# Another order of the projection products in the recurrence, twelve sums moved to GpSimd, and tiles laid out anew

## The chip, the cores and the metric

The kernel runs on one core of a Trainium2 chip. The metric is the device time of one execution in microseconds (us), of which the median of several runs is given. TensorE (PE) does matrix products, ScalarE (ACT) copies, casts and activations, VectorE (DVE) sums and products of tiles, GpSimd (POOL) a few of the same, and SyncE (SP) issues transfers. Each engine works off its own list of instructions in order; the engines meet at semaphores.

## The reference

A decoder trunk of two layers, 1024 positions of 1024 features, all float32. Cut to the part that the change touches:

```python
def hgrn2_mixer(h, w_in, lower_bound, g_norm_w, w_out):     # layer 0; 8 heads of 128
    q, f, i, g = jnp.split(h @ w_in, 4, axis=-1)            # w_in is 1024 x 4096
    fg = lb + (1.0 - lb) * jax.nn.sigmoid(heads(f))
    o = hgrn2_chunkwise(jax.nn.silu(heads(q)), 1.0 - fg, heads(i), jnp.log(fg))
    o = o * lax.rsqrt(jnp.mean(jnp.square(o), -1, keepdims=True) + RMS_EPS)
    o = o * g_norm_w * jax.nn.silu(heads(g))
    return o.reshape(B, S, D) @ w_out
...
    for layer in range(DEPTH):                              # DEPTH = 2
        mix = hgrn2_mixer(...) if layer == 0 else swa_sink_mixer(...)
        h = layer_norm(ALPHA * h + mix, ...)
        h = layer_norm(ALPHA * h + conv_ffn(h, ...), ...)
```

`hgrn2_chunkwise` is the recurrence: per head a state of 128 x 128 is decayed by `fg`, takes in key times value and is read by the query. The keys are `1 - fg`, the values are `i`, the gate is `g`.

## The kernel before

The program runs through the layers in stages: the projections and the recurrence of layer 0 (to about 500 us), its FFN, the shared keys and values with the attention of layer 1, and the second FFN. A float32 product is made of three TensorE matmuls: each operand is split into a high part (a cast on ScalarE) and a low part (the operand less its high part, `low_part`, L197), and `mm3` issues high x low, low x high and high x high as L222, L223 and L224.

**Head 0** is projected straight (values and gate at L777/L778, added up at L748 and L750). **Heads 1 to 7** are projected by a Strassen-Winograd scheme. The four projections of a head are taken in two pairs: m = 0 to 13 stands for (head, g), where g = 0 is the pair of queries and forget gates and g = 1 that of values and gates. The 1024 positions are cut into an early and a late half, and so are the features that are summed over. Each pair takes seven products P1 to P7, written (m,p), each 12 matmuls of 128x512. P2 goes to PSUM bank 1, P5 and P3 to bank 2, and P1, P6, P7 and P4 to bank 3*(m mod 2), where each of them is added onto what the bank holds. P6, P7, P3 and P4 are therefore put onto a bank that holds the product before them, and the scheme wants that product's value as well: it must be read out first. This is the work of `evacuate`: ScalarE copies P1 (L1360), P6 (L1362), P5 (L1364) and, for g = 1, P4 (L1366); VectorE adds P7, P2 and P3 to those copies (L1372), and ScalarE puts a silu over queries and gates (L1377). For g = 0, P2 and P4 are followed by `forget`, three activations on ScalarE (L1006 to L1008) that make `fg` and the keys `kp`.

The other operands are sums. Those of the input are made once: `s1` and `xf` hold sums of the transposed input, and `last_sums` (L859) casts them into the tiles T and Y (ScalarE, L866) and makes their low parts. Those of the weights are made for every pair from its two loaded tiles `raw`: sum a (L1304, L1305, ahead of P6) and sum b (L1307, L1308, ahead of P5). The weights' high parts are cast at L1285 into the tile HL, which has room for eight products.

**The recurrence of a head** lies between the products in TensorE's list. It takes, on VectorE, products over the positions (L1116 to L1124, L1105, L1107, L1110), whose results ScalarE copies (L1092 and L1093, tiles og, VG or kd); on TensorE score matmuls into psax (L228); on VectorE masked copies (L1048, L1069) into Ab; on ScalarE the copies into A (L1086, L1164); transposes of the keys and of the values on TensorE (L232), copied by ScalarE at L1174 and L1183; the matmuls of the states (L228, `psax<-VG,kd`) and the sums of the states on VectorE (L1194, L1196); and the output with its norm (L1215 to L1240).

**What sets the order.** The list of each engine is what the program issues. `product(n)` issues entry n of the list `line`, and between matmuls an `Order` object runs generators: each yields after how long it wishes to go on, by a planned time `od.t` for TensorE and `od.v` for VectorE. ScalarE and GpSimd have no planned time. `evacuate` is such a generator, started 0.3 after its product. Before a product that needs a bank, the planner runs the generators until the reader of the bank is issued. The list before:

```python
SEQ = (1, 2, 6, 5, 7, 3, 4)                                   # L1245
line = [(m, p) for m in range(len(pairs)) for p in SEQ]
for m in range(len(pairs) - 2):
    line[7 * m + 6], line[7 * m + 7] = line[7 * m + 7], line[7 * m + 6]
```

So (m,4) changes place with (m+1,1). The tiles of the heads are of the pool `hp`, whose tiles are allotted in the order in which their names are first asked for; tiles of later stages lie on the same addresses and wait until the earlier ones are free.

Of the kernel before, what the change touches and what calls it, by code (L numbers as in the profile page):

```python
# [10 lines left out]
F32 = mybir.dt.float32  # L11
# [5 lines left out]
P = 128  # L17
S = 1024
# [116 lines left out]
def trunk(ctx: ExitStack, tc: tile.TileContext, a: dict, out: bass.AP):  # L135
    nc = tc.nc
    PS = bass.MemoryType.PSUM
    od = Order()
# [56 lines left out]
    def low_part(lo, src, hi, eng):  # L195

        make = lambda e: e.tensor_tensor(lo, src, hi.bitcast(F32), op=ALU.subtract)  # L197
        if isinstance(eng, list):
            eng.append(lambda: make(nc.vector))
        else:  # L200
            return make(eng or nc.vector)
# [6 lines left out]
    def split_raw(raw, eng=None):  # L208
        ring["hl"] += 1
        return split_into(hl_at((ring["hl"] - 1) % 6), raw, eng)  # L210
# [184 lines left out]
    sub, add = ALU.subtract, ALU.add  # L395
    tt = nc.vector.tensor_tensor
# [326 lines left out]
    with tc.tile_pool(name="t", bufs=1, reuse_waits="tile") as raws, hgrn_pool as hp:  # L723
# [14 lines left out]
        def qf_split(raw, eng=None):  # L738
            return split_raw(raw, eng).rearrange("p h (k c) -> p h k c", k=KC)

        VG = {-1: hp.tile([P, 2, S], F32, name="VG", bufs=2)}
        VG[0] = hp.tile([P, 2, S], F32, name="VG", bufs=2)
        values_in, soon, gated = [-1], [], {}

        def values(tb, ps):

            vg = VG[0][:, :, tb * P:(tb + 1) * P]
            nc.scalar.copy(vg, ps[:, 256:].rearrange("p (g c) -> p g c", g=2))  # L748
# [5 lines left out]
            if tb % 2:  # L754
                G = VG[0][:, 1, (tb - 1) * P:(tb + 1) * P]
                yield 0.7
                nc.scalar.activation(G, G, AF.Silu)

        def first_values(ps):

            pv = ps.rearrange("p (t g c) -> p t g c", t=2, g=2)
            vg = VG[0][:, :, :2 * P].rearrange("p g (t c) -> p g t c", t=2)
            nc.scalar.activation(vg[:, 1], pv[:, :, 1, :], AF.Silu)
# [64 lines left out]
        A = hp.tile([P, NB, P], F32, name="A")  # L828
# [5 lines left out]
        xs = [hp.tile([P, 2, S // 2], F32, name=name, bufs=b) for name, b in (("kp", 2), ("kd", 1))]  # L834
        s1 = VG[-1].rearrange("p g (b n) -> p (g b) n", b=2)
        four = lambda t: t.rearrange("p a n -> p (a n)").rearrange("p (h k n) -> p h k n", h=2, k=4)
# [22 lines left out]
        def last_sums(part):  # L859

            for i in range(4):
                ts = slice(i * P, (i + 1) * P)
                t, src = (TXs[1][:, :, :, ts], xf[i][:, 512:]) if part else (
                    T[:, :, :4, 512 + i * P:512 + (i + 1) * P], s1[:, i])
                src = src.rearrange("p (k t) -> p k t", k=4)
                nc.scalar.copy(t[:, 0], src)  # L866
                yield od.behind(0.0, 1.0)
                low_part(t[:, 1], src, t[:, 0], None)
                od.vec(0.7)
                yield 0.1  # L870

        with tc.tile_pool(name="ep", bufs=1, reuse_waits="tile") as ep:
            pr = ep.tile([17, P], F32, name="pr")
# [161 lines left out]
        def recur(h, qs, fg, kp):  # L1035
# [53 lines left out]
            def stash(i, t):  # L1089

                halves = lambda v: v.rearrange("p (b u m) -> p b u m", u=2, m=1 << i)
                nc.scalar.copy(halves(t)[:, :, 1, :], halves(qp)[:, :, 1, :])  # L1092
                nc.scalar.copy(halves(t)[:, :, 0, :], halves(kp)[:, :, 0, :])  # L1093
                return t
# [3 lines left out]
            def update(i):  # L1098
                m = 1 << i
                nb = S // (2 * m)  # L1100
                Tm, off = level
                qv = qp.rearrange("p (b u m) -> p b u m", u=2, m=m)
                kv = kp.rearrange("p (b u m) -> p b u m", u=2, m=m)
                tv = Tm[:, off:off + 2 * nb].rearrange("p (b u) -> p b u", u=2)
                nc.vector.tensor_tensor(qv[:, :, 1, :], qv[:, :, 1, :],  # L1105
                                        tv[:, :, 0:1].to_broadcast([P, nb, m]), op=ALU.mult)
                nc.vector.tensor_tensor(kv[:, :, 0, :], kv[:, :, 0, :],  # L1107
                                        tv[:, :, 1:2].to_broadcast([P, nb, m]), op=ALU.mult)
                noff = 0 if i == 0 else off + 2 * nb
                nc.vector.tensor_tensor(tot[:, noff:noff + nb], tv[:, :, 0], tv[:, :, 1], op=ALU.mult)  # L1110
                level[:] = tot, noff
                od.vec(1.3 + nb / 700.0)
# [14 lines left out]
            update(1)  # L1127
            early = stash(2, VG[h - 1][:, 0, :] if h else hp.tile([P, S], F32, name="og"))
            yield od.behind(0.0, 0.5)
# [112 lines left out]
            if h < NH - 2:  # L1242
                nc.sync.dma_start(hod[h], G)

        SEQ = (1, 2, 6, 5, 7, 3, 4)  # L1245
        pairs = [(h, g) for h in range(1, NH) for g in range(2)]
        line = [(m, p) for m in range(len(pairs)) for p in SEQ]
        for m in range(len(pairs) - 2):
            line[7 * m + 6], line[7 * m + 7] = line[7 * m + 7], line[7 * m + 6]
        place_of = {mp: n for n, mp in enumerate(line)}  # L1250
        raw_of, landing, cast, low_made, summed_w = {}, {}, {}, set(), {}
        done, opened = [0], [0]
        order_hi = [(m, p) for m in range(len(pairs)) for p in SEQ]
        jobs = [job for m in range(len(pairs)) for job in ((m, 1), (m, "a"), (m, 2), (m, 6), (m, "b"), (m, 5), (m, 7), (m, 3), (m, 4))]

        def pair_load(m, side):
            if m < len(pairs):
                h, g = pairs[m]
                raw_of[m, side] = qf_load(h, ((1, 0), (2, 3))[g][side])
                landing[m] = od.t + 5.0  # L1260

        def source(m, p):
            r1, r2 = raw_of[m, 0], raw_of[m, 1] if (m, 1) in raw_of else None
            return {1: lambda: r1[:, :512], 2: lambda: r1[:, 512:], 6: lambda: r1[:, :512], 5: lambda: r1[:, :512],
                    7: lambda: r2[:, :512], 3: lambda: r2[:, 512:], 4: lambda: r1[:, 512:]}[p]()

        def home(n):
            return HL[:, n % 8, :].rearrange("p (h n) -> p h n", h=2)

        def cast_next(force=False):  # L1270

            if not order_hi:
                return False
            m, p = order_hi[0]
            n = place_of[m, p]
            if n - 8 >= done[0] or n >= opened[0]:
                return False
            if p in (6, 7) and (m, "a") not in summed_w or p in (5, 4) and (m, "b") not in summed_w:
                return False
            if not force and p in (6, 5) and summed_w[m, "a" if p == 6 else "b"] > od.t:  # L1280
                return False
            if (m, 0) not in raw_of or p == 3 and (m, 1) not in raw_of or not force and landing[m] > od.t:
                return False
            order_hi.pop(0)
            nc.scalar.copy(home(n)[:, 0], source(m, p))  # L1285
            cast[m, p] = od.t
            return True
# [5 lines left out]
        def job_next(force=False):  # L1293

            if not jobs:
                return False
            m, p = jobs[0]
            if p in ("a", "b"):
                if (m, 1) not in raw_of or not force and landing[m] > od.t:
                    return False  # L1300
                r1, r2 = raw_of[m, 0], raw_of[m, 1]
                b11, b21, b12, b22 = r1[:, :512], r1[:, 512:], r2[:, :512], r2[:, 512:]
                if p == "a":
                    tt(b12, b22, b12, op=sub)  # L1304
                    tt(b11, b12, b11, op=add)  # L1305
                else:
                    tt(b21, b21, b11, op=sub)  # L1307
                    tt(b11, b22, b11, op=sub)  # L1308
                od.vec(1.4, 0.0)
                summed_w[m, p] = od.v + 0.2  # L1310
            else:
                if force:
                    while (m, p) not in cast:
                        if not cast_next(True):
                            raise ValueError(f"no weights for {m} {p}")
                elif (m, p) not in cast or od.t < cast[m, p] + 1.0:
                    return False
                w = home(place_of[m, p])
                low_part(w[:, 1], source(m, p), w[:, 0], None)
                low_made.add((m, p))  # L1320
                od.vec(0.7, 0.0)
                if p == 4:
                    pair_load(m + 1, 1)
                    pair_load(m + 2, 0)
                    if m == len(pairs) - 1:
                        out_loads_first()
            jobs.pop(0)
            return True
# [82 lines left out]
        def out_loads_first():  # L1411
            for u in range(3):
                out_load(u)
# [136 lines left out]
    with (tc.tile_pool(name="ta", bufs=1, reuse_waits="tile") as raws,  # L1550
# [190 lines left out]
        with tc.manual_schedule(engines={EN.PE, EN.Activation, EN.DVE, EN.Pool}):  # L1741
# [34 lines left out]
            for c in range(8):  # L1776
                fill = q_proj(hl) if c < 7 else last_filler()
                nq, nd = next(fill)
                for bp in range(0, 4, 2):
# [7 lines left out]
                    qp = done.pop(0) if done else None  # L1787
# [93 lines left out]
```

## Time and profile before

| | |
|---|---|
| median of 3 runs | 2147.98 us (2147.77 to 2148.77) |
| the profiled execution | 2147.46 us |
| its span | 2145.7 us |
| its mean granted TensorE clock | 0.992 |
| TensorE, VectorE busy | 98%, 83% of the span |
| ScalarE, GpSimd busy | 45%, 9% |
| TensorE busy from 50 to 100 us | 38.41 of 50 us |
| TensorE busy from 200 to 400 us | 194.73 of 200 us |
| TensorE busy from 550 to 2146 us | 1584.28 of 1596 us |

The profile is of one execution. A row of an engine's sequence gives start, duration, engine, line, operation, the tile written, the tiles read and their shape; in square brackets stands how long the engine was idle before, and what it waited for last. "xN" are N instructions of one kind in a row. Matmuls overlap, so that a row's duration is longer than the distance to the next. A table of stretches gives for each stretch of time the busy time of each engine with its count of instructions, then the granted TensorE clock as a share of full speed, the share of the transfer engines and GB/s.

### The profile page before, as it was taken

How to read it: one execution, taken by the hardware profiler on the slowest of the kernel's cores; microseconds unless marked ns; L12 is line 12 of the kernel's file. 1: busy time of each engine (PE TensorE's matmuls, PEld its weight loads, DVE VectorE, ACT ScalarE, POOL GpSimd, SP SyncE). 2: the span in 40 equal slices, each digit the busy share in tenths (PEclk: the TensorE clock that was granted, in tenths of full speed). 3: DMA queues.
4: the chain of work that ended last, by engine and by line, in shares of the span. 5: the costliest groups of instructions: out<-in, count | busy, mean ns of one | idle time of the engine just before them, and what ended most of it. 6: DMA issues, size and time to landing. Idle time of an engine off the chain costs nothing. (4 is left out here: it accounts for less than half of the span.)

```text
span 2145.7 us, 31543 instructions
## 1 busy us (share of the span) xinstructions
PE 2098.1 (98%) x12303; PEld 1746.4 (81%) x12303; DVE 1778.2 (83%) x2420; ACT 968.8 (45%) x1562; POOL 189.4 (9%) x214
## 2 busy tenths in 40 slices
PE   9789999998999999999999999999999999999998
PEld 8678888877878888888888888888888888888887
DVE  6667777767999989987987858969999999978986
ACT  5455555552444444444433356742534444444430
POOL 1000000000111000100000112321010000000002
PEclk9999999999999999999999999999999999999999
DMA  4011111152228667627945611142266866449662
GB/s 151 21 50 51 50 50 50 54 188 85 92 83 203 153 179 170 158 93 239 325 156 179 180 32 38 33 138 95 82 154 171 185 165 162 125 146 325 229 206 99
DMA packets 239823, 286.82 MB, mean 134 GB/s; under 512 B 30216, under 2 KB 160440, under 8 KB 239416
## 3 DMA queue, kind: packets, MB, share of 16 engines
q1 hardware_dynamic: 223360, 238.26, 34.0%
q0 software_dynamic: 15456, 46.16, 10.9%
q8 instruction: 97, 1.59, 0.3%
q14 instruction: 54, 0.44, 0.1%
q10 hardware_dynamic: 856, 0.37, 0.1%
HBM read 241.72 MB, written 89.15 MB: 154 GB/s over the span
## 5 line engine op out<-in xcount | busy, mean ns | idle before, releaser
L222 PE MATMUL psmm<-T,HL 128*128 128x512 f32 x768 | 305.6, 398 | 5.5 <-ACT T L866 5.5
L224 PE MATMUL psmm<-T,HL 128*128 128x512 f32 x768 | 300.9, 392 | 2.4 <-DVE HL L197 2.4
L223 PE MATMUL psmm<-T,HL 128*128 128x512 f32 x768 | 300.8, 392 | 0.9 <-DVE T L197 0.9
L527 DVE SCALAR_TENSOR_TENSOR Y<-Y,cwt,Y 128x1023 f32<-128x1023 f32 (+1 forms) x176 | 225.3, 1281 | 48.6 <-ACT Y L525 47.1
L249 ACT CAST HL<-rx 128x1024 fp32r<-128x1024 f32 (+1 forms) x151 | 151.1, 1006 | 165.0 <-DMA rx<-in_ffn_w_in_dram 31.0
L197 DVE TENSOR_TENSOR HL<-rx,HL 128x1024 fp32r<-128x1024 f32 (+1 forms) x151 | 176.6, 1176 | 16.5 <-ACT HL L249 16.2
L222 PEld LDWEIGHTS psmm<-T,HL 128*128 128x128 f32 x768 | 145.2, 189 | 34.6 <-ACT T L866 5.6
L224 PEld LDWEIGHTS psmm<-T,HL 128*128 128x128 f32 x768 | 144.9, 189 | 33.8 <-DVE HL L197 3.2
L223 PEld LDWEIGHTS psmm<-T,HL 128*128 128x128 f32 x768 | 145.3, 189 | 30.4 <-DVE T L197 1.8
L525 ACT ACTIVATE Y<-Y,cwt 128x1024 f32<-128x1024 f32 x88 | 108.8, 1237 | 93.4 <-DVE Y L514 82.9
L222 PE MATMUL psax<-T,HL 128*128 128x512 f32 x352 | 137.7, 391 | 0.0
L223 PE MATMUL psax<-T,HL 128*128 128x512 f32 x352 | 137.2, 390 | 0.0
L224 PE MATMUL psax<-T,HL 128*128 128x512 f32 x352 | 137.2, 390 | 0.0
L197 DVE TENSOR_TENSOR HL<-raw,HL 128x512 fp32r<-128x512 f32 (+1 forms) x121 | 91.9, 788 | 25.5 <-ACT HL L1285 13.6
L271 POOL TENSOR_TENSOR rs<-rs,nhalf 128x1 f32<-128x1 f32 x32 | 45.0, 1407 | 737.6 <-DVE rs L270 737.6
L249 ACT CAST HT<-rx 128x1024 fp32r<-128x1024 f32 (+1 forms) x37 | 35.6, 961 | 136.1 <-DVE rx L481 61.8
L222 PE MATMUL psmm<-HL 128*128 128x512 f32 x220 | 87.2, 397 | 7.8 <-ACT qs L1362 6.5
L223 PE MATMUL psmm<-HL 128*128 128x512 f32 x220 | 85.9, 390 | 0.0
L224 PE MATMUL psmm<-HL 128*128 128x512 f32 x220 | 85.8, 390 | 0.0
L249 ACT CAST HL<-Y 128x1024 fp32r<-128x1024 f32 (+1 forms) x32 | 28.5, 892 | 109.1 <-DVE Y L481 44.5
L222 PEld LDWEIGHTS psax<-T,HL 128*128 128x128 f32 x352 | 66.1, 188 | 14.3 <-DVE Y L508 0.4
L224 PEld LDWEIGHTS psax<-T,HL 128*128 128x128 f32 x352 | 66.1, 188 | 13.7
(392 smaller groups left out, 5404.5 us busy)
## 6 DMA issues: line engine op xcount, KB each, us to landing
rx<-in_ffn_w_in_dram SPq DMA_DIRECT2D x136, 256.0 KB
rx<-gd SPq DMA_DIRECT2D x118, 256.0 KB
bsd<-in_ffn_w_out_dram POOLq DMA_DIRECT2D x36, 768.0 KB, 8.5
gd<-Y SPq DMA_DIRECT2D x44, 512.0 KB
raw<-in_hgrn_w_in_dram SPq DMA_DIRECT2D x30, 512.0 KB
rx<-in_ffn_w_out_dram SPq DMA_DIRECT2D x54, 256.0 KB
R<-bsd SPq DMA_DIRECT2D x44, 256.0 KB
Y<-in_ffn_w_in_dram SPq DMA_DIRECT2D x40, 256.0 KB
```

The source lines that it names most:

```text
L197: make = lambda e: e.tensor_tensor(lo, src, hi.bitcast(F32), op=ALU.subtract)
L222: nc.tensor.matmul(ps, st(0), mv(0), start=start, stop=False, skip_group_check=onto)
L223: nc.tensor.matmul(ps, st(0), mv(1), start=False, stop=False, skip_group_check=onto)
L224: nc.tensor.matmul(ps, st(1), mv(0), start=False, stop=stop, skip_group_check=onto)
L249: nc.scalar.copy(hi, src)
L271: nc.gpsimd.tensor_tensor(rs, rs, nhalf, op=ALU.pow)
L525: nc.scalar.activation(c, u, AF.Identity, bias=cwt[:, l, 3, ci:ci + 1], scale=cwt[:, l, 2, ci:ci + 1])
L527: nc.vector.scalar_tensor_tensor(c[:, sh:], u[:, :S - sh], cwt[:, l, 2 - sh, ci:ci + 1], c[:, sh:], op0=ALU.mult, op1=ALU.add)
```

## The change

Four things are changed.

1. **The list of products.** The first pair begins as before with P1, P2, P6, P5, P7. For each next pair m the list goes on with (m,1), (m-1,3), (m-1,4), (m,6), (m,5), (m,2), (m,7). Between two products of one bank now stand two others (three between P5 and P3) where one stood. (m,4) keeps its place. The last pair keeps its old order.
2. **The low parts of `last_sums`,** eight of 128x512 (four into T, four into Y), go from VectorE to GpSimd, and the casts are issued 0.8 of the planner's time apart, no longer behind VectorE's planned time.
3. **The sums a and b of the first pair,** four of 128x512, go from VectorE to GpSimd; the planner takes them as done 3.0 later.
4. **The pool `hp`.** The tiles fg, qs, kp, kd, tot, St, qp, A and og are asked for first, VG after them, so all have other addresses.

Two lines are added ahead of these places, so L866 becomes L868, L1304 becomes L1305, L1360 to L1377 become L1362 to L1379.

```diff
+        for name, copies in (("fg", 1), ("qs", 1), ("kp", 2), ("kd", 1), ("tot", 1), ("St", 1), ("qp", 1), ("A", 1), ("og", 1)):
+            hp.tile([P, S], F32, name=name, bufs=copies)
         VG = {-1: hp.tile([P, 2, S], F32, name="VG", bufs=2)}
...
                 nc.scalar.copy(t[:, 0], src)
-                yield od.behind(0.0, 1.0)
-                low_part(t[:, 1], src, t[:, 0], None)
-                od.vec(0.7)
-                yield 0.1
+                low_part(t[:, 1], src, t[:, 0], nc.gpsimd)
+                yield 0.8
...
-        SEQ = (1, 2, 6, 5, 7, 3, 4)
         pairs = [(h, g) for h in range(1, NH) for g in range(2)]
-        line = [(m, p) for m in range(len(pairs)) for p in SEQ]
-        for m in range(len(pairs) - 2):
-            line[7 * m + 6], line[7 * m + 7] = line[7 * m + 7], line[7 * m + 6]
+        line = [(0, 1), (0, 2), (0, 6), (0, 5), (0, 7)]
+        for m in range(1, len(pairs) - 1):
+            line += [(m, 1), (m - 1, 3), (m - 1, 4), (m, 6), (m, 5), (m, 2), (m, 7)]
+        line += [(len(pairs) - 2, 3), (len(pairs) - 2, 4)] + [(len(pairs) - 1, p) for p in (1, 2, 6, 5, 7, 3, 4)]
...
+                make = nc.vector.tensor_tensor if m else nc.gpsimd.tensor_tensor
                 if p == "a":
-                    tt(b12, b22, b12, op=sub)
-                    tt(b11, b12, b11, op=add)
+                    make(b12, b22, b12, op=sub)
+                    make(b11, b12, b11, op=add)
                 else:
-                    tt(b21, b21, b11, op=sub)
-                    tt(b11, b22, b11, op=sub)
-                od.vec(1.4, 0.0)
-                summed_w[m, p] = od.v + 0.2
+                    make(b21, b21, b11, op=sub)
+                    make(b11, b22, b11, op=sub)
+                if m:
+                    od.vec(1.4, 0.0)
+                summed_w[m, p] = od.v + 0.2 if m else od.t + 3.0
```

How it moves instructions shows at three places. First GpSimd's list around the first products, before and then after; Y_462 and T are the tiles of the input's sums, raw_113 and raw_114 those of the weights.

```order
L904 DMA pr<-in_hgrn_lb_logits_dram 16x128
L905 DMA pr<-in_hgrn_gnorm_w_dram 1x16x8
L197 TENSOR_TENSOR HL<-raw_112,HL 128x1024
L1223 TENSOR_SCALAR ss<-ss 128x8
L1224 TENSOR_TENSOR ss<-ss,nhalf 128x8
```

```order
L197 TENSOR_TENSOR HL<-raw_112,HL 128x1024
L197 TENSOR_TENSOR Y_462<-St,Y_462 128x4x128
L197 TENSOR_TENSOR Y_462<-qp,Y_462 128x4x128
L197 TENSOR_TENSOR Y_462<-tot,Y_462 128x4x128
L197 TENSOR_TENSOR Y_462<-og,Y_462 128x4x128
L1305 TENSOR_TENSOR raw_114<-raw_114 128x512
L1306 TENSOR_TENSOR raw_113<-raw_114,raw_113 128x512
L197 TENSOR_TENSOR T<-VG,T 128x4x128 x2
L1308 TENSOR_TENSOR raw_113<-raw_113 128x512
L1309 TENSOR_TENSOR raw_113<-raw_114,raw_113 128x512
L197 TENSOR_TENSOR T<-VG,T 128x4x128 x2
```

The twelve stand in one run; sum b (L1308, L1309) follows two of T's low parts.

Second, ScalarE's list from the copy of P1 of the first pair to the copies of P6 and P5, before and then after.

```order
L1285 CAST HL<-raw_113 128x512
L1360 COPY fg<-psmm 128x512
L1285 CAST HL<-raw_114 128x512 x2
L1285 CAST HL<-raw_113 128x512
L1285 CAST HL<-raw_112 128x512 x2
L866 CAST T<-VG 128x4x128
L1092 COPY kd<-qp 128x8x64
L1093 COPY kd<-kp 128x8x64
L1086 COPY A<-psax 32x8x32 x2
L1164 COPY A<-Ab 32x8x32 x4
L866 CAST T<-VG 128x4x128 x2
L1362 COPY qs<-psmm 128x512
```

```order
L1285 CAST HL<-raw_112 128x512
L868 CAST T<-VG 128x4x128
L1092 COPY kd<-qp 128x8x64
L1093 COPY kd<-kp 128x8x64
L1086 COPY A<-psax 32x8x32 x2
L1164 COPY A<-Ab 32x8x32 x4
L1006 ACTIVATE fg<-fg 128x512
L1007 ACTIVATE fg<-fg,lbt 128x512
L1008 ACTIVATE kp<-fg,one 128x512
L1364 COPY qs<-psmm 128x512
L1366 COPY qs<-psmm 128x512
```

Two casts of T left the place ahead of P6's copy, and the three activations of `forget` came there.

Third, ScalarE's list in the recurrence of head 2, beside the products of pair 4, from the copies into A to the copy of the transposed values (L1183 in both), before and then after.

```order
L1164 COPY A<-Ab 32x8x32 x4
L1362 COPY qs<-psmm 128x512
L1006 ACTIVATE fg<-fg 128x512
L1007 ACTIVATE fg<-fg,lbt 128x512
L1008 ACTIVATE kp<-fg,one 128x512
L1364 COPY qs<-psmm 128x512
L1086 COPY A<-psax 64x8x64
L1174 COPY kd<-psax 128x1024
L1183 COPY VG<-psax 128x1024
```

```order
L1366 COPY qs<-psmm 128x512
L1285 CAST HL<-raw_114 128x512
L1086 COPY A<-psax 64x8x64
L1174 COPY kd<-psax 128x1024
L1006 ACTIVATE fg<-fg 128x512
L1007 ACTIVATE fg<-fg,lbt 128x512
L1008 ACTIVATE kp<-fg,one 128x512
L1379 ACTIVATE qs<-qs 128x512
L1285 CAST HL<-raw_114 128x512
L1183 COPY VG<-psax 128x1024
```

P6's copy (L1364 after) went ahead of the copies into A and does not stand here any more; `forget`, a silu and a cast now stand between L1174 and L1183.

More of the change, by code (lines that the diff above doesn't have):

```diff
@@ L1252, in trunk @@
         done, opened = [0], [0]
-        order_hi = [(m, p) for m in range(len(pairs)) for p in SEQ]
+        order_hi = [(m, p) for m in range(len(pairs)) for p in (1, 2, 6, 5, 7, 3, 4)]
         jobs = [job for m in range(len(pairs)) for job in ((m, 1), (m, "a"), (m, 2), (m, 6), (m, "b"), (m, 5), (m, 7), (m, 3), (m, 4))]
```

## The prediction

> **What bounds the kernel now.** I read the page's first part, then TensorE's waits, then the table of stretches, then the engines' own sequences where TensorE waited. The page:
>
> ```profile
> PE 2098.1 (98%) x12303; PEld 1746.4 (81%) x12303; DVE 1778.2 (83%) x2420; ACT 968.8 (45%) x1562; POOL 189.4 (9%) x214
> ```
>
> TensorE is the bound, and the change neither adds nor removes one of its products. So it can only win back idle time and time at a low clock, and only where it touches the order. TensorE's waits from 62 to 500 us, its stretch from the first product of heads 1 to 7 on (label, total us, times, longest):
>
> ```profile
> PE psmm L222 <- ACT qs L1362: 6.5, 5, 1.3
> PE psmm L222 <- ACT T L866: 5.5, 1, 5.5
> PE psmm L222 <- ACT fg L1360: 3.9, 1, 3.9
> PE psmm L222 <- ACT qs L1364: 3.5, 1, 3.5
> PE psmm L224 <- DVE HL L197: 2.8, 2, 2.2
> PE psmm L222 <- ACT VG L1362: 1.3, 1, 1.3
> ```
>
> L1360, L1362 and L1364 are the copies of P1, P6 and P5 out of a PSUM bank on which the next product of that bank must be put: 15.2 us in 8 waits. The table by stretches shows that the clock was lost as well (PEclk is the number ahead of the last two):
>
> ```profile
> 50.00:100.00 50.00, 38.41 (x429) 30.42 (x428) 32.18 (x60) 21.00 (x41) 0.00 (x0) 0.90 0.08 22
> 150.00:200.00 50.00, 48.02 (x497) 40.18 (x498) 35.92 (x65) 25.01 (x54) 3.22 (x2) 0.97 0.17 53
> ```
>
> TensorE's own sequence in the first of them:
>
> ```profile
> 65.42 0.50 PE L224 MATMUL psmm<-T,HL 128*128 128x512 f32 x1 [2.19 <-DVE HL L197]
> 77.15 0.50 PE L222 MATMUL psmm<-Y,HL 128*128 128x512 f32 x1 [3.91 <-ACT fg L1360]
> 78.22 0.63 PE L223 MATMUL psmm<-Y,HL 128*128 128x512 f32 x1
> 81.69 0.70 PE L228 MATMUL psax<-kd 128*32 128x16 f32 x62
> 82.26 0.67 PE L228 MATMUL psax<-qp,kp 128*32 128x32 f32 x31
> 88.41 0.80 PE L222 MATMUL psmm<-T,HL 128*128 128x512 f32 x1 [5.47 <-ACT T L866]
> 91.88 0.40 PE L223 MATMUL psmm<-T,HL 128*128 128x512 f32 x1
> 458.16 2.20 PE L1506 MATMUL psmm<-HL,T 128*128 128x512 f32 x9
> ```
>
> The first three idle gaps belong to products (0,1), (0,6) and (0,5). Nine matmuls in a row took 2.20 (the last row), a start every 0.225; a row's own time is longer, since they overlap. From 78.22 to 81.69 and from 88.41 to 91.88 a matmul took 0.63 (0.80 at first) instead of 0.40: 3.47 us each at about half pace, so some 1.7 us lost each. The same followed the 3.5 us wait for L1364 (the 0.97 of 150 to 200): 1.7 more. So within the order's reach lie 11.6 us of waits and 3.4 of clock in the start, and 11.9 (6.5 + 3.5 + 1.3 + 0.6) and 1.7 in the later heads: 28.6 us, the ceiling of the main theory. TensorE's other waits there are not of this order and stay.
>
> **GpSimd's share of the start.** Eight low parts and four sums leave VectorE. By the groups (mean ns of one):
>
> ```profile
> L197 DVE TENSOR_TENSOR T<-VG,T 128x512 fp32r<-128x512 f32 x4 | 2.7, 686 | 1.4 <-ACT T L866 1.4
> L1675 POOL TENSOR_TENSOR X<-X,bf 128x512 f32<-128x512 f32 x32 | 41.2, 1287 | 54.1 <-DVE X L1667 52.5
> ```
>
> So VectorE sheds 12 x 0.69 = 8.3 us, and GpSimd gets 12 x 1.29 = 15.5 us where it did nothing (0.00 from 50 to 100). Neither matters by itself; what matters is who waits:
>
> ```profile
> 51.51 0.60 ACT L1033 ACTIVATE qs<-psmm 128x512 f32<-128x512 f32 x1 [2.20 <-PE psmm L224]
> 52.64 0.69 DVE L197 TENSOR_TENSOR Y<-og,Y 128x512 fp32r<-128x512 f32 x1 [2.53 <-ACT Y L866]
> 64.68 0.69 DVE L197 TENSOR_TENSOR HL<-raw,HL 128x512 fp32r<-128x512 f32 x1
> 76.00 0.62 ACT L1285 CAST HL<-raw 128x512 fp32r<-128x512 f32 x1 [4.38 <-DVE raw L1308]
> 76.52 0.58 ACT L1360 COPY fg<-psmm 128x512 f32<-128x512 f32 x1
> 77.00 2.70 ACT L1285 CAST HL<-raw 128x512 fp32r<-128x512 f32 x5
> 87.22 1.14 ACT L866 CAST T<-VG 128x512 fp32r<-128x512 f32 x2
> ```
>
> (0,1): VectorE no longer stands 2.53 us for the cast of the last Y sum before head 0's recurrence. It can begin when q is ready, at 52.1 (51.51 + 0.60) instead of 53.3, about 1.1 us earlier, so the low part of 64.68 comes at about 63.6 and the wait falls from 2.19 to 1.1. (0,6): P1's copy stood behind a cast that stood behind VectorE's sum b. On GpSimd the sum's last piece follows the low part of 63.6 (its end 64.3) and three sums and two low parts, 5 x 1.29: 70.8; the casts of T (0.62 each, between) hold the two low parts back to about 72. Then cast and copy, 0.52 + 0.58: 73.1 instead of 77.1. TensorE, 1.1 us earlier too, is there at 72.1: a wait of about 1.3 with the semaphores instead of 3.91. (0,5): its T casts were third and fourth behind five casts and head 0's copies (87.22). Now the four casts are spread and the last is done near 76.3, its low part on GpSimd at 77.5; TensorE comes at 77.5. Wait 5.47 to 0.
>
> (0,7) is the new place. P6's copy now stands behind the forget chain L1006 to L1008, all behind head 0's copies of kd and A:
>
> ```profile
> 83.75 0.62 ACT L1092 COPY kd<-qp 128x512 f32<-128x512 f32 x1 [3.53 <-DVE qp L1105]
> 85.56 1.64 ACT L1164 COPY A<-Ab 32x256 f32<-32x256 f32 x4
> 255.17 0.58 ACT L1362 COPY qs<-psmm 128x512 f32<-128x512 f32 x1
> 255.78 0.63 ACT L1006 ACTIVATE fg<-fg 128x512 f32<-128x512 f32 x1
> 257.92 0.56 ACT L1364 COPY qs<-psmm 128x512 f32<-128x512 f32 x1
> ```
>
> The score matmuls ended at 82.93; the copies begin 0.8 later (83.75), take 3.45 (to 87.20), the chain 2.14 (255.78 to 257.92), the copy 0.58: 7.0 us after the scores. TensorE has 18 matmuls of 0.225 between: 4.1. The wait is 2.9; bounds 0 (should ScalarE be ahead) and 4.2 with 1.7 of clock. Behind (0,7) on TensorE stand head 0's 16 score matmuls and the transposes of kd, so the recurrence waits with it.
>
> VectorE and GpSimd also held each other up where both ran:
>
> ```profile
> 618.74 3.78 POOL L532 TENSOR_TENSOR Y<-Y 128x1024 f32<-128x1024 f32 x1 [44.12 <-DVE Y L527]
> 619.02 1.23 DVE L197 TENSOR_TENSOR HL<-rx,HL 128x1024 fp32r<-128x1024 f32 x1
> 627.07 2.41 POOL L532 TENSOR_TENSOR Y<-Y 128x1024 f32<-128x1024 f32 x1 [4.56 <-DVE Y L527]
> 627.42 2.60 DVE L481 TENSOR_TENSOR Y<-Y,rx 128x512 f32<-128x512 f32 x1
> ```
>
> One GpSimd operation took 3.78 instead of 2.41, ending 2.3 after VectorE's; one VectorE operation took 2.60 instead of 0.69, ending 0.5 after GpSimd's. That is a whole block, not a slowdown. Such pairs will meet between 50 and 78 us, since head 0's recurrence is made of two-tile operations. Bounds: 0, if the twelve fall into gaps, and 6.7 as worked out in the first rival; I take 2.0, nearer to the low end, since VectorE was busy for 32.18 of these 50 us before and now sheds 8.3 of them: GpSimd finds gaps.
>
> The Trainium skill, "SBUF — State Buffer", section "Who interferes with whom", says just this: a VectorE instruction with both inputs in SBUF and a GpSimd instruction that reads SBUF exclude each other, and the second to issue blocks fully. The trace agrees (2.60 for 0.69). By this rule no meeting is free, and the sum would lean to the first rival.
>
> Start: 11.6 + 3.4 - (1.1 + 1.3 + 0 + 2.9 + 2.0) = 7.7 us won.
>
> **The order of the products.** Two products, 5.5 us, now lie between a product and the next of its bank, instead of one, 2.7 us. The waits on P6 were 1.3 each, because the copy came at 255.17 behind A's copies; with another 2.7 us they go. The 3.5 on P5, and the 0.6 behind, go too: 11.9 + 1.7. What is late next: the second product of a pair comes two places later, so its forget chain now stands between the transposes of kd and those of V, ahead of the copy L1183 on which the states' matmuls wait:
>
> ```profile
> 260.25 1.01 ACT L1174 COPY kd<-psax 128x1024 f32<-128x1024 f32 x1 [0.44 <-PE psax L232]
> 263.87 1.02 ACT L1183 COPY VG<-psax 128x1024 f32<-128x1024 f32 x1 [2.61 <-PE psax L232]
> 262.80 1.03 PE L232 MATMUL psax<-ident,VG 128*128 128x128 f32 x8
> 265.06 1.73 PE L228 MATMUL psax<-VG,kd 128*128 128x128 f32 x14
> ```
>
> Before, ScalarE had 2.61 us of idle ahead of L1183, and TensorE did not wait at 265.06. Now ScalarE has 0.1 + 0.9 (L1174) + 2.14 (forget) + 1.08 (a silu and a cast, at the pace of five in 2.70) + 1.02 (L1183) = 5.2, in some heads 0.5 more for P1's copy, against 18 matmuls and 8 transposes on TensorE, 4.1 + 1.0 = 5.1. With 0.2 of semaphores the wait is 0.3 to 0.8; I take 0.5 in six heads: 3.0. Bounds 0 and 1.3 each. Later heads: 13.6 - 3.0 = 10.6 won.
>
> **The tiles.** Addresses change which transfer waits for which release at the end of the stage. No instruction after the recurrence moves. TensorE's longest wait from 500 to 720 us:
>
> ```profile
> PE psmm L232 <- DVE Y L283: 4.8, 1, 4.8
> ```
>
> It ends with VectorE's chain of layer norms, whose last input is the recurrence's own last output: 0 taken, bounds 0 and 6.5 (4.8 and 1.7 of clock).
>
> **Sum.** 7.7 + 10.6 = 18.3 us. The profiled execution took 2147.46 (span 2145.7), 0.5 below the median of 2147.98: 2147.5 - 18.3 = 2129.
>
> **The rivals.**
> 1. Full blocking between VectorE and GpSimd. Both at 64.3 and in the two triples of L1105, L1107 and L1110 ahead of the scores: (0,1) waits 3.1, (0,6) 4.5, and the clock falls as at 77.15, 1.7: 2.0 + 3.0 + 1.7 in place of 2.0, so 2134. For it: the two rows. Against: the third of the stretch that VectorE leaves free.
> 2. New waits eat more. (0,7) waits 4.2 and loses 1.7 of clock (3.0 more), and each head 1.3 at its states (4.8 more): 2137. For it: ScalarE's and TensorE's sums are within 0.1 us. Against: ScalarE is 45% busy.
> 3. The waits only move: what leaves the P6 copies comes back at the states, what leaves (0,5) at (0,7): 2147. Against: they would have to match by chance in both stages.
> 4. Slower. The one mechanism is the copy L1183 behind the forget chain, which itself waits for VectorE's sum of P2. Without states waits the gain is 21.3, so it decides from 3.55 us a head in six heads; at that length the clock falls too, as it did behind L1364: 6 x (3.55 + 1.7) = 31.5, so 10.2 slower, 2158. For it: the chain is as long as its cover, so every us by which that sum is late shows in full. Against: VectorE makes it as soon as P2 is done, and would have to be 3 us late in every head.
> 5. The new addresses also free the FFN's entry (6.5 more): 2123.
>
> The Trainium skill, "TensorE: Matmul & The Clock Gate", section "What's actually happening", puts the fall to half clock at an idle window of about 3.4 us that runs free. The rows agree for 3.91 and 5.47 (slow for 3.47 behind them) and for 2.19 (none). By it the 2.9 at (0,7) stays free of charge, and 1.7 more falls due if it passes 3.4.
>
> **How the numbers follow.** Main case 0.50 (its own range 2123 to 2135, by the bounds of the new waits), first rival 0.15, second 0.15, third 0.08, fourth 0.07, fifth 0.05. A change of 0.2% (4.3 us) is about what a measurement here can tell from none. Faster: 0.50 + 0.15 + 0.14 + 0.05 = 0.84; the same: 0.08 + 0.01; slower 0.07. The range reaches from 2119 (the ceiling, 28.6) to 2143; it leaves out the third and fourth rival.
>
> **What would show it.** TensorE's waits on L1362 and L1364 (two lines on in the changed file) at 120, 152, 203 to 413 us gone; one of about 2.9 on P6's copy near 80; waits of 0.3 to 0.8 on L1183, six times; granted clock of 50 to 100 us near 1.00. GpSimd operations of over 1.4 us, or VectorE's L1105 at over 0.8, are the blocking. Wrong if the waits on L1183 pass 1.3, or if TensorE's idle time between 62 and 500 us, 28 us now, stays above 18.

## The result, and the profile after

The changed kernel takes 2133.69 us (median of 4 runs, 2132.9 to 2134.82) beside 2148.38 of the kernel before on the same chip: the ratio is 0.993, with a 95% interval of 0.9913 to 0.9948. That is 14.7 us faster. The forecast was 2129, 19 us faster, with a range of 2119 to 2143. The profiled execution's span fell from 2145.7 to 2131.1, and this is what the following rows split up.

TensorE's waits from 62 to 500 us after the change (who waited, for whom: total us, times, longest):

```profile
PE psmm L222 <- ACT qs L1364: 6.0, 2, 5.4
PE psmm L224 <- DVE HL L197: 2.8, 1, 2.8
PE psax L228 <- ACT VG L1183: 2.3, 4, 0.7
PE psmm L222 <- ACT fg L1362: 2.2, 1, 2.2
PE psmm L222 <- ACT T L249: 1.0, 1, 1.0
PE psax L232 <- DVE og L1226: 1.0, 1, 1.0
PE psax L232 <- ACT A L1086: 0.7, 1, 0.7
PE psax L228 <- issue: 0.5, 1, 0.5
PE psmm L1508 <- ACT T L1433: 0.5, 1, 0.5
```

The waits of the later heads on P6 and P5 are gone but for 0.7; the new one on L1183 is there, 0.7 in three heads and 0.2 in a fourth. TensorE's idle time from 62 to 500 us, 28 us before, is 17.0 by these rows. What stays large is the start. TensorE's sequence there, and the stretches:

```profile
66.27 0.50 PE L224 MATMUL psmm<-T,HL 128*128 128x512 f32 x1 [2.81 <-DVE HL L197]
76.32 0.50 PE L222 MATMUL psmm<-Y,HL 128*128 128x512 f32 x1 [2.21 <-ACT fg L1362]
88.82 0.80 PE L222 MATMUL psmm<-HL 128*128 128x512 f32 x1 [5.35 <-ACT qs L1364]
89.41 0.63 PE L223 MATMUL psmm<-HL 128*128 128x512 f32 x1
```

```profile
50.00:100.00 50.00, 39.62 (x449) 31.78 (x448) 34.60 (x56) 22.13 (x44) 15.68 (x11) 0.97 0.08 22
150.00:200.00 50.00, 50.00 (x509) 41.85 (x508) 39.14 (x70) 25.65 (x59) 3.00 (x2) 1.00 0.18 54
```

(0,1) waits 2.8 (2.2 before), (0,6) 2.2 (3.9), (0,5) not at all (5.5), and (0,7), which did not wait before, 5.4: 10.4 us in place of 11.6, with one spell of half clock in place of two. So the start won about 3 us, and most of the rest was won in the later heads.

GpSimd and VectorE in the start, after the change: GpSimd's rows first, then VectorE's.

```profile
53.09 2.29 POOL L1305 TENSOR_TENSOR raw<-raw 128x512 f32<-128x512 f32 x1
69.22 2.53 POOL L197 TENSOR_TENSOR T<-VG,T 128x512 fp32r<-128x512 f32 x2 [1.25 <-ACT T L868]
71.70 1.75 POOL L1308 TENSOR_TENSOR raw<-raw 128x512 f32<-128x512 f32 x1
73.53 1.60 POOL L1309 TENSOR_TENSOR raw<-raw,raw 128x512 f32<-128x512 f32 x1
78.94 1.68 POOL L197 TENSOR_TENSOR T<-VG,T 128x512 fp32r<-128x512 f32 x1 [2.42 <-ACT T L868]
```

```profile
54.15 2.31 DVE L1117 TENSOR_TENSOR qp<-qs,fg 128x1024 f32<-128x1024 f32 x1
70.51 1.78 DVE L1105 TENSOR_TENSOR qp<-qp,tot 128x512 f32<-128x512 f32 x1 [1.17 <-PE psax L228]
72.22 1.78 DVE L1107 TENSOR_TENSOR kp<-kp,tot 128x512 f32<-128x512 f32 x1
73.92 1.29 DVE L1110 TENSOR_TENSOR tot<-tot 128x64 f32<-128x64 f32 x1
78.75 2.42 DVE L197 TENSOR_TENSOR HL<-raw,HL 128x512 fp32r<-128x512 f32 x2
```

Each of these VectorE rows is longer by about 1.1 than before (L1117 1.22, L1105 and L1107 0.69, L1110 0.22, a low part 0.69 or 1.3 for two). With L1116 (0.6) and one low part at 46.51 us (1.1), GpSimd held VectorE up for 7.2 us, while it had taken 8.3 us of work off it.

### The profile page after: what moved, and what is told of

It reads as the page before. It is cut to its first block, busy times and chain, and to the rows that moved or that the text cites. A ratio compares the mean times of both kernels' runs of the same rounds, so it can differ in the third digit from the quotient of the medians.

```text
span 2131.1 us, 31572 instructions
## 1 busy us (share of the span) xinstructions
PE 2093.3 (98%) x12303; PEld 1743.4 (82%) x12303; DVE 1777.7 (83%) x2408; ACT 968.5 (45%) x1562; POOL 205.1 (10%) x226
## 5 line engine op out<-in xcount | busy, mean ns | idle before, releaser
L197 DVE TENSOR_TENSOR HL<-rx,HL 128x1024 fp32r<-128x1024 f32 (+1 forms) x151 | 176.6, 1176 | 18.6 <-ACT HL L249 18.3
```

## The experiments

**The theory** after this reading (A): nearly all of the gain is the new list's, in the later heads; in the start, VectorE is freed of 8.3 us and blocked for 7.2, and what is late there is ScalarE's queue behind it. **The rival** (B): the parts need each other, or the twelve operations on GpSimd are themselves what won. All times are medians of 4 or 5 runs, except 11 for the tiles; the kernel before stood at 2147.1 to 2148.2 in these groups. The runs of one kernel spread by 0.6 to 7.3 us, so that a difference of 1 or 2 us between two medians is not clear of noise. TensorE's waits are read for each kernel from its one trace.

### One part at a time

The new list alone (the change's `line` in the kernel before; cut to its beginning):

```diff
+        line = [(0, 1), (0, 2), (0, 6), (0, 5), (0, 7)]
+        for m in range(1, len(pairs) - 1):
+            line += [(m, 1), (m - 1, 3), (m - 1, 4), (m, 6), (m, 5), (m, 2), (m, 7)]
...
```

> The new list of products alone; low parts and first sums on VectorE, tiles where they were. Theory A (nearly all of the gain is the list's, and lies behind 100 us; the start is a draw between casts freed and VectorE and GpSimd blocking each other): the waits for P6's and P5's copies at 120 to 413 us are gone, 0.7 for L1183 in four heads, and at the start the old waits of about 2.2, 3.9 and some 5 us stay; 2135, that is 12 to 13 us faster than before. Rival B (the two parts belong together, the list needs the freed VectorE): under 6 us faster, 2142 or more.

Measured: 2135.01, ratio 0.9935 (0.9923 to 0.9948), 13.2 us faster. Its waits on TensorE from 50 to 500 us:

```profile
PE psmm L222 <- ACT T L866: 5.5, 1, 5.5
PE psmm L222 <- ACT fg L1360: 3.9, 1, 3.9
PE psax L228 <- ACT VG L1183: 2.7, 5, 0.7
PE psmm L224 <- DVE HL L197: 2.2, 1, 2.2
```

The start is as before to 0.1 us, and in the later heads no wait on a copy of P6 or P5 is left, only the new ones on L1183: A holds. By the medians the other parts add 1.3 us, which is within the noise.

GpSimd's twelve operations alone:

> The eight low parts and the first four sums on GpSimd alone; old list, old tiles. Theory A: a few us at the start only (the wait for the casts of T, 5.5, shrinks, but VectorE's products in head 0's recurrence are blocked for about 1 us each, and P6's copy is as late): 2143 to 2147. Every later wait of 1.3 stays. Rival B: 5 us or more faster, 2142 or less.

Measured: 2141.32, ratio 0.9965 (0.9951 to 0.9979), 6.9 us faster, more than A had put it at and what B had asked for (5 us or more). TensorE waits 2.8, 1.8, 0.3 and 4.1 in the start, 2.5 us less than before, but also hardly any longer in head 1 (0.2), where before it lost 1.3, 0.6 and 3.5 and 1.7 of clock, about 7 us. Against that, the wait on P6's copy in head 2 grew from 1.3 to 3.0 (at 196 us) and half clock followed it, which gives back 3.3. So some 4 us of what this part wins behind the start are waits that the list takes away as well. That is most of why 13.2 and 6.9 make 14.7 together and not 20.1. Why head 1 comes free without the new list was not tried.

The tiles alone:

> The new addresses alone. Both theories: no change within 0.1%, 2147 to 2149; TensorE's wait of 4.8 on L283 at the FFN's entry stays within 0.6.

Measured: 2148.31, ratio 1.0002 (0.9993 to 1.001). The wait on L283 is 5.4, not shorter. The new addresses are worth nothing that eleven runs could show. In this trace the wait on "issue" near 453 us is 0.2 in place of 2.0, but a spell of half clock stands near 66 us, where the kernel before had none.

### Undoing one part of GpSimd's work

The low parts back on VectorE, the sums stay on GpSimd:

```diff
-                low_part(t[:, 1], src, t[:, 0], nc.gpsimd)
-                yield 0.8
+                yield od.behind(0.0, 1.0)
+                low_part(t[:, 1], src, t[:, 0], None)
+                od.vec(0.7)
+                yield 0.1
```

> The changed kernel with the eight low parts back on VectorE and the casts paced as before; the first four sums stay on GpSimd. Theory A (blocking costs what the freed VectorE brings): VectorE's rows L1116, L1117, L1105 and L1107 between 52 and 75 us go back from 1.8 to 2.3 to 0.7 to 1.2, except beside a sum; the wait of 5.35 at (0,7) falls to 3 or less, the wait at (0,5) for the casts of T comes back in part; 2131 to 2136. Rival (the low parts on GpSimd are a clear gain): 2138 or more.

Measured: 2134.93, ratio 0.9936 (0.9923 to 0.9948). VectorE's three rows that stood at 1.78, 1.78 and 1.29 in the changed kernel (here two lines further on):

```profile
71.49 0.69 DVE L1107 TENSOR_TENSOR qp<-qp,tot 128x512 f32<-128x512 f32 x1 [2.16 <-PE psax L228]
72.10 0.68 DVE L1109 TENSOR_TENSOR kp<-kp,tot 128x512 f32<-128x512 f32 x1
72.70 0.22 DVE L1112 TENSOR_TENSOR tot<-tot 128x64 f32<-128x64 f32 x1
```

With GpSimd's rows beside them gone, VectorE is at full pace: the blocking is shown. (0,6) and (0,7) do not wait at all; instead (0,5) waits 4.8 for T's last cast, which is late again, and a product at 136 us waits 2.3 for VectorE. A's time holds. By the medians the low parts on GpSimd are worth 1.2 us in this order of things, which is within the noise.

The sums back on VectorE, the low parts stay on GpSimd:

```diff
-                make = nc.vector.tensor_tensor if m else nc.gpsimd.tensor_tensor
+                make = nc.vector.tensor_tensor
-                if m:
-                    od.vec(1.4, 0.0)
-                summed_w[m, p] = od.v + 0.2 if m else od.t + 3.0
+                od.vec(1.4, 0.0)
+                summed_w[m, p] = od.v + 0.2
```

> The changed kernel with the first pair's four sums back on VectorE; the eight low parts stay on GpSimd. Theory A (blocking): VectorE has four operations more and GpSimd four fewer between 53 and 75 us; where GpSimd's sums blocked VectorE's L1117 (2.3 for 1.2) and L1105, L1107 (1.8 for 0.7), these go back, but P1's copy waits for VectorE's sum b again, so (0,6) waits 2 to 4: 2132 to 2137. Rival (the sums on GpSimd are what won the start): (0,6) waits 4 or more and the time is 2137 or more.

Measured: 2130.3 (2128.75 to 2130.68), ratio 0.9916 (0.9902 to 0.993). This is better than both had it, and 3.4 us better than the changed kernel. Its start, and two rows of ScalarE:

```profile
64.66 0.50 PE L224 MATMUL psmm<-T,HL 128*128 128x512 f32 x1 [1.70 <-DVE HL L197]
78.10 0.79 PE L222 MATMUL psmm<-Y,HL 128*128 128x512 f32 x1 [5.63 <-ACT fg L1360]
89.11 0.50 PE L222 MATMUL psmm<-HL 128*128 128x512 f32 x1 [1.35 <-ACT qs L1362]
88.48 0.59 ACT L1362 COPY qs<-psmm 128x512 f32<-128x512 f32 x1
89.09 0.63 ACT L1006 ACTIVATE fg<-fg 128x512 f32<-128x512 f32 x1
```

L1117 is back at 1.21, so (0,1) waits 1.1 less than in the changed kernel. (0,6) waits 5.6, more than the 2 to 4 that A had expected, since P1's copy stands behind the cast of sum b: here the rival's bound of 4 was right, though not its time. (0,7) waits 4.0 less. That isn't the sums' own doing alone: with this edit the three forget activations came to stand behind P6's copy (L1362 here) in ScalarE's list (the two rows), and not ahead of it as in the changed kernel; VectorE's low parts were also made before the scores. When (0,7) starts the clock is up again. Of the 4.0 us between the two profiled executions 2.0 are there at the FFN's entry; 1.6 more come in the next 104 us, where the edit changed nothing, but the half clock lasted 3.4 in place of 6.8 us. So the four sums on GpSimd won nothing; how much they cost by themselves these runs don't show.

### ScalarE's queue

The forget activations of the first pair's early half 3 later, that is behind the copies of P6 and P5:

```diff
                 elif g == 0:
+                    yield 3.0 if m == 0 else 0.0
                     forget(h, first, kp, half, to[:, half])
```

> The changed kernel, with the three forget activations of the first pair's early half issued 3 of the planner's time later, behind the copies of P6 and P5 and of the transposed keys; nothing else. Theory A (the wait of 5.35 at (0,7) is ScalarE's queue: 2.2 of it these activations, the rest the copies of kd, late because of blocked VectorE): the wait falls to about 3.1 and the clock keeps up or nearly so: 2 to 4 us faster than the changed kernel, 2130 to 2132. Rival (the copy waits for something else, the activations lie in its shadow): 2133 to 2135, the wait over 4.8.

Measured: 2130.9 (2127.42 to 2134.76), 2.8 us less than the changed kernel by the medians, though its runs reach as high as that kernel's. The wait decides:

```profile
87.78 0.65 PE L222 MATMUL psmm<-HL 128*128 128x512 f32 x1 [3.10 <-ACT qs L1364]
```

The wait at (0,7) fell by 2.25, which is what the three activations take. So they did stand ahead of P6's copy, as the prediction had it, and the remaining 3.1 is the rest of the queue. TensorE reached (0,7) 1.2 us later here, behind a spell of half clock at 67.5 us, and head 0's scores and copies are later by as much; the difference of the waits is free of that.

The same in all heads (`yield 3.0`), which puts them behind L1183 as well:

> As the run before, and in the later heads the same three activations also 3 later, behind the copy L1183 of the transposed values. Theory A (the waits of 0.7 at the states are these activations ahead of L1183): the four waits on L1183 go, 2.3 us or some more less than the run before, 2127 to 2130. Rival (they only move, to the next head's first products on VectorE or to the casts behind): no more than 0.5 us less than the run before.

Measured: 2127.92 (2125.76 to 2130.19), ratio 0.9906 (0.9893 to 0.992). That is 3.0 us less than the run before by the medians, though the runs overlap. No wait on L1183 is left in its trace, and from 200 to 400 us TensorE is busy throughout (197.66 of 200 us in the run before):

```profile
200.00:400.00 200.00, 200.00 (x2020) 167.48 (x2019) 154.47 (x278) 113.51 (x246) 9.31 (x8) 1.00 0.18 55
```

So the new waits at the states were the activations ahead of L1183. A part comes back further on: 0.4 at L1196 and 0.5 more at L1226, at 414 and 431 us.

The same with the low parts on VectorE (T's 1.0 behind their casts, Y's paced as before):

> As the run before, and the eight low parts back on VectorE, Y's paced as before, T's 1.0 behind their casts without regard to VectorE's planned time; the sums stay on GpSimd. Theory A (with only four operations on GpSimd little is blocked, and T's casts are no longer late): waits of 2.2 at (0,1), about none at (0,6), 2 to 3 at (0,5) or (0,7), clock near 1.00 in 50 to 100 us: 2123 to 2128. Rival (VectorE with the low parts is late again): (0,5) waits 4 or more, 2129 or more.

Measured: 2129.34 (2128.42 to 2130.01), the rival's time, not A's. Both expectations are half right: 2.2 and 0.9 at (0,1) and (0,6), and little blocking (VectorE's L1110, L1105 in the changed kernel, takes 1.66 for 0.69 and a low part 1.22 beside the sums), but 3.3 at (0,5), where T's last low part is late on VectorE.

### A version that beats both

The last four runs put ScalarE's copies of the first pair as early as they can be, and make (0,1)'s low part, whose cast was done over 9 us before it in the changed kernel, inside VectorE's first chain of head 0. Low parts on GpSimd, sums on VectorE, the forget activations 3 later in all heads, and beside these edits, shown above:

```diff
             readers[b] = od.spawn(evacuate(m, p, ps, taken), 0.3), taken
+            if m == 0 and p in (1, 6, 5):
+                od.step(readers[b][0])
...
             cast[m, p] = od.t
+            if (m, p) == (0, 1):
+                od.later(0.9, lambda: job_next(True))
```

> From the changed kernel: the eight low parts on GpSimd, the four sums on VectorE, the forget activations later in all heads, P1's, P6's and P5's copies of the first pair issued as soon as their product is, and product (0,1)'s low part made 0.9 behind its cast, inside head 0's first VectorE chain. Theory A (ScalarE's queue and that low part make the start's waits): (0,1) under 1, (0,6) under 1.5, (0,7) under 1.5, none at L1183; 2121 to 2126. Rival (VectorE, blocked by GpSimd's low parts, is what is late, in whatever order the copies stand): the start's waits still sum to over 6 and the time is 2127 or more.

Measured: 2120.96 (2120.49 to 2121.22), ratio 0.9875 (0.9858 to 0.9891): 26.8 us faster than the kernel before and 12.7 below the changed one. (0,1), (0,5) and (0,7) do not wait, and nothing waits on L1183. (0,6) does, twice as long as A had allowed it:

```profile
73.64 0.80 PE L222 MATMUL psmm<-Y,HL 128*128 128x512 f32 x1 [3.12 <-ACT fg L1362]
```

The same with the low parts on VectorE and the sums on GpSimd:

> The same, but with the low parts on VectorE and the four sums on GpSimd. Theory A: only four operations on GpSimd, so VectorE's rows in head 0 go back to 0.7 and 1.2 except beside a sum, no wait at (0,6); TensorE's scores of head 0 come later, since T's low parts lie ahead of them on VectorE; 2120 to 2126. Rival (GpSimd has to take the low parts): 2127 or more.

Measured: 2123.51, ratio 0.9887 (0.9873 to 0.9902), as A expected, with no wait at (0,6). In the start stand waits of 0.6, 0.6 and 3.8, the last for a low part of T on VectorE.

The same with nothing on GpSimd:

> The same with nothing at all on GpSimd: low parts and sums on VectorE, in the new order of copies. Theory A (freeing VectorE of 12 operations is worth next to nothing, since GpSimd blocks VectorE for as long; what counts is the order on ScalarE): within 3 us of the better of the two runs before. Rival (the twelve on GpSimd are worth what VectorE sheds, some 8 us of a chain on which TensorE waits): 5 us or more slower than the better of the two.

Measured: 2128.67, ratio 0.9914 (0.9899 to 0.9929), 7.7 us slower than the first of these. Here the rival is right. Its trace from 50 to 500 us (cut to the waits that the first of these doesn't have):

```profile
PE psmm L222 <- DVE VG L1379: 2.8, 1, 2.8
PE psmm L222 <- ACT T L868: 2.6, 1, 2.6
PE psmm L223 <- DVE T L197: 2.3, 1, 2.3
PE psmm L224 <- DVE HL L197: 0.8, 1, 0.8
```

With ScalarE's queue out of the way, VectorE is what is late (2.3 and 2.8 us at (0,5) and at 183 us, and 0.8 at 115 us), and handing a part of its work to GpSimd is worth 5 (the four sums) or 8 us (the eight low parts), blocking included. Both together in this order were not tried.

P1's copy earlier still, ahead of the copies of head 0's results on ScalarE:

```diff
-                od.tick()
-            done[0] = n + 1
-            taken = []
-            readers[b] = od.spawn(evacuate(m, p, ps, taken), 0.3), taken
+                if k == 3:
+                    taken = []
+                    readers[b] = od.spawn(evacuate(m, p, ps, taken), 0.3), taken
+                    if m == 0 and p in (1, 6, 5):
+                        od.step(readers[b][0])
+                od.tick()
+            done[0] = n + 1
```

> As run y2, with P1's copy issued right behind the twelfth matmul of (0,1), which puts it ahead of the copies of head 0's blocked VectorE results on ScalarE (L1092, L1093). Theory A (the 3.1 at (0,6) is the queue on ScalarE, behind results of VectorE that GpSimd's low parts and sum b hold up): that wait falls to under 1 with its 1.6 of clock, some of it coming back before (0,5) or at the scores, which still need the blocked VectorE: 2116 to 2119. Rival (the whole chain is bound by blocked VectorE, so the wait only moves to the low parts or the scores): within 1.5 us of 2121.

Measured: 2121.5, ratio 0.9879 (0.9863 to 0.9896), no better. The wait went from (0,6) to (0,5), for T's cast and its low part on GpSimd:

```profile
76.51 0.50 PE L222 MATMUL psmm<-T,HL 128*128 128x512 f32 x1 [3.02 <-ACT T L868]
77.85 0.80 PE L223 MATMUL psmm<-T,HL 128*128 128x512 f32 x1 [0.84 <-POOL T L197]
```

T's last cast stands behind five casts of weights and these behind the copies of L1105's and L1107's results, which VectorE makes behind two sums that GpSimd blocks (1.79 and 1.67 us for 0.69). So here the rival holds: what is left is that chain, and moving a copy on ScalarE only moves the wait.

## Why the prediction was right, and where it was wrong

The direction, the range and the place of most of the gain were right; the size was 3.7 us too large, 18.3 against 14.6 in the profiled span. In the start 7.7 us were forecast and 3.0 won.

- **The later heads: right.** 13.6 less 3.0 was forecast. The waits on P6, P5 and the low part behind fell by 11.2 and the clock's 1.7 came back; the waits on L1183 are 2.3. That is 10.6, as forecast; that it agrees so closely is luck, since 0.7 stayed at a copy of P6 and 0.7 less came on L1183. The 0.2 "of semaphores" in that term was an allowance: the rows show 0.04 from one engine's end to the next one's start (263.83 to 263.87). The list alone showed all of it, and the run with the activations behind L1183 showed that the 2.3 have the cause that was named.
- **The tiles: right,** nothing.
- **(0,5): right,** no wait, though narrowly. T's last low part was done at 80.62 and not at 77.5, and TensorE, late itself, came to the matmul that reads it at 80.81.
- **(0,7): the mechanism on ScalarE was right, the size wrong.** 2.9 was forecast, 5.35 came. ScalarE's rows after the change:

```profile
82.45 0.62 ACT L1092 COPY kd<-qp 128x512 f32<-128x512 f32 x1 [3.59 <-DVE qp L1105]
84.27 1.65 ACT L1164 COPY A<-Ab 32x256 f32<-32x256 f32 x4
85.92 0.63 ACT L1006 ACTIVATE fg<-fg 128x512 f32<-128x512 f32 x1
88.18 0.59 ACT L1364 COPY qs<-psmm 128x512 f32<-128x512 f32 x1
```

  The copies took 3.47 (3.45 forecast), the activations 2.26 (2.14). The step that failed is "the copies begin 0.8 later": they began 3.3 after the scores had ended (78.47 + 0.67 = 79.14 us), since in VectorE's list two low parts (2.42) and the sum of P2 (L1374, 0.67) stood ahead of L1105. Of these 2.5 us 1.1 is the block by GpSimd's last low part; 1.4 is VectorE's own order, which the prediction had not priced.
- **(0,1) and (0,6): wrong by the block.** Head 0's recurrence did start 0.8 earlier (52.43), but L1116 and L1117 took 1.7 longer beside GpSimd, and 2.81 came for 1.1. At (0,6) 2.21 came for 1.3.
- **The term that failed is the blocking, "I take 2.0".** What came in its place is 1.7 at (0,1), 0.9 at (0,6), 2.5 at (0,7) and some 1.6 of clock behind the last: 6.7, of which the 1.4 of VectorE's order are not blocking. The bound above was 6.7 and the first rival 2134. That both were met is partly luck, as the rival had put 4.5 at (0,6) (4.3 by its own sum) and nothing more at (0,7). The reasoning "GpSimd finds gaps" is what failed. The twelve operations did not stand in the third of the time that VectorE left free; the casts and sums that released them stood next to VectorE's own chains. The Trainium skill, "SBUF — State Buffer", section "Who interferes with whom", had said that an operation with both inputs in SBUF and a GpSimd operation that reads SBUF exclude each other, and the trace agrees row for row (1.78 for 0.69).
- **What offset it was luck:** the wait of 2.0 on "issue" at 453 us, taken as staying, is gone (0.5 stands elsewhere in this trace), and the clock behind it did not fall: with small changes beside it some 2.1 us that were not forecast. In the traces of the single parts it is 1.8 with GpSimd's part alone, 0.2 with the tiles alone and none with the list alone. What it is was not settled. Behind the recurrence 0.9 was lost, at the FFN's entry. Start 3.0 (1.2 of waits and 1.8 of clock), later heads 10.6, these 2.1, less 0.9: 14.8 beside the measured 14.6.

## What to carry to other kernels

Where an engine in order makes results for a bottleneck, price an edit by what stands in that engine's queue ahead of the result after the edit: here each new wait was such a queue. The one on L1183 was priced to 0.2 us; the one at (0,7) was missed by 2.5, because the queue of the engine before it, VectorE, was left out. Do not count work handed to GpSimd as free when VectorE's operations beside it read two tiles from SBUF: check for each pair whether they can meet, and charge it to one of them (here some 1.1 us a time). Do not take it as worthless either: with ScalarE's queue out of the way it won 5 to 8 us. And parts of a change that remove the same waits don't add up: 13.2 and 6.9 us made 14.7.

## What the runs showed of the hardware beyond that

VectorE and GpSimd took turns. In the kernel before, GpSimd was kept out by two VectorE operations in a row (3.78 us for 2.41); after the change three VectorE operations in a row each waited for one of GpSimd's (1.78, 1.78 and 1.29 us), and GpSimd's between them took 1.75 and 1.60 in place of 1.28. So neither has a lasting right of way.

The clock fell behind shorter waits than the prediction reckoned with. The Trainium skill, "TensorE: Matmul & The Clock Gate", section "What's actually happening", has an idle window of about 3.4 us that runs free. Here the same wait at the same matmul left the clock up in the run with the list alone and halved it in the run with the low parts back:

```profile
65.18 0.50 PE L224 MATMUL psmm<-T,HL 128*128 128x512 f32 x1 [2.18 <-DVE HL L197]
```

```profile
65.74 0.79 PE L224 MATMUL psmm<-T,HL 128*128 128x512 f32 x1 [2.18 <-DVE HL L197]
66.33 0.63 PE L222 MATMUL psmm<-T,HL 128*128 128x512 f32 x1
```

That the window runs free fits this; that it takes 3.4 us of idleness does not. In each trace all changes of the clock fall on a grid of 3.413 us, which starts elsewhere in each (with the low parts back they come at 65.75, 69.16, 82.81, 89.64, 137.43 and 140.84 us between 60 and 500 us). Here are two stretches of that grid for each of the two runs, the list alone first, with TensorE's busy time and the clock:

```profile
63.42:66.83 3.41, 1.65 (x7) 1.00 0.02 5
66.83:70.24 3.41, 3.41 (x158) 1.00 0.00 0
62.34:65.75 3.41, 1.23 (x8) 1.00 0.00 0
65.75:69.16 3.41, 3.41 (x11) 0.50 0.02 5
```

The wait of 2.18 lay with 1.75 in one stretch and 0.43 in the one before in the first run, and whole in one stretch in the second. The traces of these 14 kernels hold 8618 such stretches at full clock. The clock is halved behind each of the 70 in which TensorE was idle for 0.53 or more, that is 1.8 us, and behind none in which it was idle for 0.52 or less. So a wait of 2.2 us is not safe, and shorter waits in one stretch add up: behind the 3.0 above one matmul ran at full pace, and after 0.8 more of idle time the next ran at half (0.80). It is also a likely reason why one kernel's runs spread by up to 7 us, which was not shown. Of the five runs from 2127.42 to 2134.76 the fastest had a mean granted clock of 0.998 and the slowest one of 0.993, but the fifteen runs of the kernel before, from 2144.77 to 2150.19, show no such order.
